# FFN-in of a hybrid backbone layer: sums of products accumulated in PSUM, weight sums and low parts on VectorE, the gate's g·sigmoid(g) as one ScalarE function

## The chip, the cores and the metric

The kernel runs on one core of one Trainium2 chip. The metric is device microseconds of one execution. Three runs of the kernel before took 1524.94, 1530.69 and 1537.96 us; their median, 1530.69 us, is the time before. All profile rows come from one profiled execution with a span of 1529.1 us.

## The reference, cut to what matters

One layer of a trunk over 512 latent tokens (and 256 context tokens) of width 1024, in float32. Three token mixers come first and end in an output projection. Then comes the sub-layer that the change touches, and a last RMSNorm:

```
def _swiglu(h, w_in, w_out):
    g, u = jnp.split(h @ w_in, 2, axis=-1)
    return (jax.nn.silu(g) * u) @ w_out

h_lat = _rmsnorm(x_lat, norm_ffn_w[l]) * (1.0 + sc2) + sh2
x_lat = x_lat + g2 * _swiglu(h_lat, w_ffn_in[l], w_ffn_out[l])
```

The hidden width is 2816, so w_in is 1024 x 5632 and gives 22 blocks of 128 columns of g and 128 of u.

## The kernel before, in words

Every float32 product is made of three TensorE products in the faster float32r type: a value is split into a high part (a cast, by ScalarE) and a low part (value minus high part, a subtraction), and high·high, high·low and low·high are summed in PSUM.

FFN-in (in `run`, from L1735 on) treats the 22 blocks of columns in two ways. The first two (FC = 2) are plain products (`halves`). The other 20 use a scheme of Strassen's kind with seven products instead of eight. A block's weights are four quadrants A11, A12, A21, A22 of 128 x 512 (the columns of g or of u by half of the channels); the tokens come in quadrants too, and sums of token quadrants are made once (`token_sums`). For each block the four weight quadrants are loaded by DMAs (L1628, issued on SP's queue), `weight_sums` makes S1 to S4 from them (L1635), and `part` splits each of the seven left operands with a cast (L1806, ScalarE) and a low part (L1807). Which engine makes the sums is given by `FE1`, which makes the low parts by `FE2`, in the order of the products; before, all four sums and two low parts of seven are on GpSimd (G), five low parts on VectorE (V).

`prepare` is a generator that is advanced once after each product. It makes the sums about a block ahead and the split of the product that stands FD = 4 places further on. The split parts and weights live in 23 slots (`wslot`, `wput`), taken in the order in which they were freed; a DMA into a slot waits for the slot's last reader.

`product` (L1842) runs 12 matmuls of 256 columns on TensorE, four channel blocks by three parts, into a PSUM bank. In the kernel before each of the seven products starts a bank of its own, and the sums that the scheme needs afterwards are VectorE's: ScalarE copies the first product to SBUF (L1858), VectorE adds the others in seven additions of 128 x 256 (L1859 to L1866), six of which read PSUM. Then `gate` (L1766) computes silu(g)·u: ScalarE's Tanh of g/2 (L1769), and two VectorE operations with a scalar and two tensors each (L1770, L1772). Blocks from FE0 = 4 on are split into high and low parts only after the loop (L362, L363), in tiles that held the tokens and the activations before; earlier ones at once. Then FFN-out starts (L1884).

TensorE runs its instructions in the order in which the code is written. For the other engines the tile framework plans the order, by the order of the code and by what its plan believes to be ready; each engine then runs that order strictly, and an instruction that waits holds all behind it on its engine. The framework places all waits, those for a buffer's last reader too.

Of the kernel before, what the change touches and what calls it, by code (L numbers as in the profile page):

```python
# [9 lines left out]
F32 = mybir.dt.float32  # L10
# [4 lines left out]
OP = mybir.AluOpType  # L15
# [25 lines left out]
KV = 6  # L41
# [15 lines left out]
FE1 = "GGGG"  # L57
FE2 = "VVGVVGV"
# [34 lines left out]
class Slots:  # L93
    """A unit's share of the working tiles of phase one; what it puts back it can take again."""
# [18 lines left out]
    def pieces(self, c):  # L113
        """A tile of class c, cut into tiles of 512 columns."""
        t = self.get(c)
        return [t[:, j:j + 512] for j in range(0, SIZE[c] - 511, 512)]
# [11 lines left out]
    def close(self, *keep):  # L128
        """Everything is given back but for the tiles kept."""
        names = {t.tensor.name for t in keep}  # L130
        for n in [n for n in self.out if n not in names]:
            c, i = self.out.pop(n)
            self.net.free[c].append(i)
        for c, z in self.own.items():
            self.net.free[c].extend(z)
            z.clear()


class Net:
# [18 lines left out]
    def crow(self, name, n):  # L158
        """A row of constants on every partition."""
        t = self.cp.tile([128, n], F32, name="c_" + name)  # L160
        self.dma(t, self.a[name].unsqueeze(0).to_broadcast([128, n]))
        return t
# [36 lines left out]
    def block(self, key):  # L199
        """The weight block of a key, split; fetched before if it was announced."""  # L200
        if key not in self.wcache:
            self.fetch(key)
        for f in self.wcache[key][3]:
            f()
        self.wcache[key][3].clear()
        return self.wcache[key][:2]

    def fetch(self, key, now=True, pieces=None):
        """Starts to load a weight block, or some pieces of it; gives the functions that split them."""
# [35 lines left out]
    def jobs(self, queue, gens=None, then=()):  # L245
        """Runs jobs (weight block, function, ...) in order, the next block on its way, and
        carries the scans on between them."""
# [36 lines left out]
    def ready(self):  # L284
        """The next job: of those that can run, the first whose weights are here."""
        z = self.upcoming()
        if not z:
            return None
        if z[0][0] is not None and z[0][0] not in self.wcache:
            z = [y for y in z if y[0] and y[0][0] in FILL and y[0] in self.wcache] + z  # L290
        return self.queue.index(z[0])

    def push(self, jobs):
        """Jobs to be run next, behind those of the block that is on its way."""
        i = max((n + 1 for n, z in enumerate(self.queue) if z[0] in self.wcache), default=0)
        self.queue[i:i] = jobs
# [15 lines left out]
    def dense(self, *parts, ks=None):  # L312
        """parts: (PSUM, weights, first column, last, tokens (high, low), first, last)."""
# [23 lines left out]
    def load_x(self):  # L337
        """The residual stream, where the context was."""
# [8 lines left out]
    def tok(self, W, i):  # L347
        """Tokens of tile i (context 0, 1, latents 2..5) on partitions, 256 columns."""
# [23 lines left out]
    def rstd_gen(self, sq, n, scale, cb, rb):  # L372
        """1 / rms of n tokens, on every partition (in rb), from tiles of squares."""
# [25 lines left out]
    def silu_c(self, c):  # L399
        """c (1 + tanh(c / 2)) of the two modulation vectors, on every partition; rows of 128, an  # L400
        identity behind them."""
# [18 lines left out]
    def modulate(self, k, s, silu):  # L420
        """Shift and scale of channels 128 k .. of one vector, by VectorE."""
# [14 lines left out]
    def modulate_pe(self, sc, ws):  # L436
        """Shift and scale of the channels from 128 KV of both vectors, by TensorE."""
# [20 lines left out]
    def scale_in(self, x, n, s, k, H, L, rb, eng):  # L458
        """The modulated norm of channels 128 k .., split."""
# [13 lines left out]
    def conv(self, acc, p, n, w, cc):  # L473
        """SAME convolution of 5 taps over the free axis, scaled by 1/2."""
# [16 lines left out]
    def gates(self):  # L491
        """Columns: decays of the SSD heads, forward and backward (32), of the mLSTM heads (8); the
        latter's input gates behind them. Tokens on partitions, tiles 0, 1 context, 2..5 latents."""
# [154 lines left out]
    def turn_rows(self, own, R, E, n, name):  # L648
        """Two sets of columns as rows over the latents, in DRAM."""
# [379 lines left out]
    def head_turn(self, own, ht, w, columns):  # L1029
        """Channels of a head on partitions, times the norm's gain; from column to row order."""  # L1030
# [257 lines left out]
    def prepare(self, b, Y, H, L, own):  # L1288
        """Splits the output of branch b, channels as they come."""
# [100 lines left out]
    def rstd2(self, c):  # L1390
        """1 / rms of 256 tokens from c on, from the sums of squares."""
# [4 lines left out]
    def late(self):  # L1396
        """The rest of the modulation of the latents."""
# [18 lines left out]
    def startup(self):  # L1416
        """The modulated inputs, and block after block of their channels the first products."""
# [144 lines left out]
    def add_square(self, m, x, c0, c1):  # L1562
        """Adds block m of the channels to the sum of squares, the last one kept apart."""
# [8 lines left out]
    def scale2(self, c, sv, h):  # L1572
        """The modulated norm before the FFN of 256 tokens from c on, in h and split."""
# [15 lines left out]
    def token_sums(self, h):  # L1589
        """With B11, B12 / B21, B22 the quadrants (channels, tokens) of h: T1 = B12 - B11,  # L1590
        T2 = B22 - T1, T3 = B22 - B12 and T4 = B21 - T2, split; per pair of channel blocks
        the tiles (T1, T3) and (T4, T2)."""
# [17 lines left out]
    def weight_sums(self, f, out):  # L1610
        """The quadrants (columns, channels) A11, A12 / A21, A22 of an FFN block and
        S1 = A21 + A22, S2 = S1 - A11, S3 = A11 - A21, S4 = A12 - S2, in steps."""
# [27 lines left out]
    def aup(self, up):  # L1640
        """The decays' weights of a head, three times: their low parts once and the high ones twice."""
# [5 lines left out]
    def small(self, p, c0, c1):  # L1647
        """The rows of the decays, three times: their high parts twice and the low ones."""
# [5 lines left out]
    def first(self, Y):  # L1654
        """Ends the products of the startup: the rows of the gates, the first GLA head's q and k."""
# [20 lines left out]
    def run(self):  # L1676
# [19 lines left out]
        with pool("hx") as self.hp:  # L1696
# [45 lines left out]
            with pool("sp3") as sp, pool("fp") as fp:  # L1742
# [12 lines left out]
                def split(f):  # L1755
                    """An early block in tiles of its own, a late one where h and the block before were."""
# [9 lines left out]
                def gate(f, g, u):  # L1766
                    """silu(g) u"""
                    t = sp.tile([128, 512], F32, name="ft", bufs=2)
                    S.activation(t, g, AF.Tanh, scale=0.5)  # L1769
                    V.scalar_tensor_tensor(t, t, 1.0, g, op0=OP.add, op1=OP.mult)  # L1770
                    act[f] = t if f < FE0 else fp.tile([128, 512], F32, name=f"a{f}")
                    V.scalar_tensor_tensor(act[f], t, 0.5, u, op0=OP.mult, op1=OP.mult)  # L1772
# [4 lines left out]
                order = ("A11", "S2", "S1", "A12", "S3", "A22", "S4")  # L1777
# [4 lines left out]
                def prepare():  # L1782
                    """Sums and splits of the weights, one step ahead of each product."""
# [29 lines left out]
                def halves():  # L1813
                    """The first FFN blocks, half of the tokens after the other."""
# [27 lines left out]
                def product(f, n, dst):  # L1842
                    dst = dst[:, :256]
                    H, L, slots = parts.pop(7 * (f - FC) + order.index(n))
                    for k in range(4):
                        h, l = B[n][k]
                        w, v = H[:, 128 * k:128 * k + 128], L[:, 128 * k:128 * k + 128]
                        for j, (x, y) in enumerate(((w, h), (w, l), (v, h))):
                            T.matmul(dst, x, y, start=(k == 0 and j == 0), stop=(k == 3 and j == 2))  # L1849
                    self.wput(*slots)  # L1850
                    next(prep, None)
                    return dst

                for f in range(FC, KF):
                    lo, hi = slice(0, 256), slice(256, 512)
                    g, u = (sp.tile([128, 512], F32, name=n, bufs=2) for n in ("fg", "fu"))
                    m, r, v = (sp.tile([128, 256], F32, name=n, bufs=2) for n in ("fm", "fr", "fv"))
                    S.copy(m, product(f, "A11", self.acc_bank()))  # L1858
                    V.tensor_add(r, m, product(f, "S2", self.bank()))  # L1859
                    p5 = product(f, "S1", self.bank())  # L1860
                    V.tensor_add(g[:, lo], m, product(f, "A12", self.acc_bank()))
                    V.tensor_add(g[:, hi], r, p5)
                    V.tensor_add(v, r, product(f, "S3", self.bank()))
                    V.tensor_add(u[:, hi], v, p5)
                    V.tensor_add(u[:, lo], v, product(f, "A22", self.acc_bank()))
                    V.tensor_add(g[:, hi], g[:, hi], product(f, "S4", self.bank()))  # L1866
                    gate(f, g, u)
# [46 lines left out]
    def final(self, c):  # L1914
        """The last norm of 256 tokens from c on; the gain is in but for the last block of channels."""
# [4 lines left out]
        for h in range(4):  # L1920
            o = self.sp.tile([128, 2, 256], F32, name=("ft", "fu")[h % 2], bufs=2)
# [34 lines left out]
def lay_out(i):  # L1956
# [43 lines left out]
    # constants of the shapes alone  # L2000
# [29 lines left out]
```

## Time and profile before

| | |
|---|---|
| median of three runs | 1530.69 us (1524.94 to 1537.96) |
| span of the profiled execution | 1529.1 us |
| TensorE (PE) busy | 1406.8 us, 92% |
| VectorE (DVE) busy | 1033.0 us, 68% |
| ScalarE (ACT) busy | 644.0 us, 42% |
| GpSimd (POOL) busy | 587.2 us, 38% |
| mean granted TensorE clock | 0.973 of full speed |

The shares are means over stages. A matmul counts as busy from its start to a modelled end, and matmuls overlap: one of 256 columns is listed with some 0.28 us, while the next starts 0.118 us later. So TensorE's speed is read from the count of matmuls in a stretch, not from the busy time. In the same way a VectorE or ScalarE instruction's listed time overlaps the next one's; the spacing of starts is what an instruction costs in a full queue.

### The profile page before, as it was taken

How to read it: one execution, taken by the hardware profiler on the slowest of the kernel's cores; microseconds unless marked ns; L12 is line 12 of the kernel's file. 1: busy time of each engine (PE TensorE's matmuls, PEld its weight loads, DVE VectorE, ACT ScalarE, POOL GpSimd, SP SyncE). 2: the span in 40 equal slices, each digit the busy share in tenths (PEclk: the TensorE clock that was granted, in tenths of full speed). 3: DMA queues.
4: the chain of work that ended last, by engine and by line, in shares of the span. 5: the costliest groups of instructions: out<-in, count | busy, mean ns of one | idle time of the engine just before them, and what ended most of it. 6: DMA issues, size and time to landing. Idle time of an engine off the chain costs nothing.

```text
span 1529.1 us, 22249 instructions
## 1 busy us (share of the span) xinstructions
PE 1406.8 (92%) x8044; PEld 1204.6 (79%) x8044; DVE 1033.0 (68%) x1783; ACT 644.0 (42%) x1191; POOL 587.2 (38%) x465
## 2 busy tenths in 40 slices
PE   5898999999999999998997789899998888888997
PEld 3687889887788886887796767677798888887887
DVE  7958463869684658786666765435369999999332
ACT  4464464553244443334454443333355343436231
POOL 4423432324222123221226353134457888881011
PEclk9998999999999999999999999999989999999999
DMA  6532323233443234354455566666322233223331
GB/s 258 189 105 84 106 69 97 72 97 97 137 126 103 78 96 129 88 129 127 159 173 171 175 210 211 197 201 215 117 77 83 83 94 100 84 84 113 90 90 66
DMA packets 99022, 190.39 MB, mean 125 GB/s; under 512 B 10752, under 2 KB 19472, under 8 KB 97760
## 3 DMA queue, kind: packets, MB, share of 16 engines
q1 hardware_dynamic: 98912, 188.97, 39.8%
q8 instruction: 63, 1.03, 0.3%
q14 instruction: 47, 0.39, 0.1%
HBM read 167.27 MB, written 21.14 MB: 123 GB/s over the span
## 4 chain that ended last, share of the span: by engine, by line
PE 53%; DVE 19%; DMA 8%; issue 6%; ACT 5%; POOL 4%; SPq 0%; DVEq 0%; ACTq 0%; POOLq 0%
PE acc L318 28%; PE acc L1884 7%; PE acc L357 7%; DVE w L1807 6%; DMA w<-in_w_main_dram 4%; PE bank L318 2%; DVE ft L1770 2%; DMA w<-in_w_b_dram 1%; ACT w L1806 1%; ACT w L215 1%; DVE w L217 1%; DMA t<-in_wmodT_dram 1%; PE bank L974 1%; POOL row L1160 1%; DMA gd<-xk 1%
## 5 line engine op out<-in xcount | busy, mean ns | idle before, releaser
L217 POOL TENSOR_TENSOR w<-w,w 128x512 fp32r<-128x512 f32 x125 | 176.2, 1409 | 572.8 <-ACT w L215 499.4
L318 PE MATMUL acc<-hlh,w 128*128 128x512 f32 (+1 forms) x1160 | 390.7, 406 | 5.5 <-ACT hlh L465 1.9
L215 ACT CAST w<-w 128x512 fp32r<-128x512 f32 (+1 forms) x302 | 183.2, 613 | 382.9 <-DMA w<-in_w_main_dram 182.6
L217 DVE TENSOR_TENSOR w<-w,w 128x512 fp32r<-128x512 f32 x177 | 138.6, 785 | 202.7 <-ACT w L215 168.6
L318 PEld LDWEIGHTS acc<-hlh,w 128*128 128x128 f32 x1160 | 225.3, 194 | 59.9 <-ACT hlh L465 2.2
L318 PE MATMUL acc<-hll,w 128*128 128x512 f32 (+1 forms) x576 | 230.7, 400 | 3.7 <-DVE hll L471 1.5
L1635 POOL TENSOR_TENSOR w<-w,w 128x512 f32<-128x512 f32 x80 | 135.7, 1717 | 2.7 <-DMA w<-in_w_ffs_dram 1.9
L318 PEld LDWEIGHTS acc<-hll,w 128*128 128x128 f32 x576 | 111.8, 194 | 28.7 <-DVE hll L471 1.9
L1807 DVE TENSOR_TENSOR w<-w,w 128x512 fp32r<-128x512 f32 x100 | 124.0, 1241 | 0.0
L318 PE MATMUL acc<-t,w 128*128 128x512 f32 x440 | 111.2, 401 | 7.4 <-DVE t L363 2.7
L318 PEld LDWEIGHTS acc<-t,w 128*128 128x128 f32 x440 | 83.2, 190 | 28.9 <-DVE t L363 4.3
L1806 ACT CAST w<-w 128x512 fp32r<-128x512 f32 x140 | 79.1, 618 | 60.9 <-DVE w L1807 50.2
L357 PE MATMUL acc<-w,hlh 128*128 128x256 f32 x512 | 96.6, 289 | 0.0
L1849 PE MATMUL bank<-th,w 128*128 128x256 f32 x480 | 93.4, 283 | 0.1
L1849 PE MATMUL acc<-hlh,w 128*128 128x256 f32 x280 | 59.6, 290 | 29.9 <-DVE w L1807 29.9
L357 PEld LDWEIGHTS acc<-w,hlh 128*128 128x128 f32 x512 | 81.6, 194 | 3.0 <-ACT t L920 1.6
L480 DVE SCALAR_TENSOR_TENSOR cacc<-acc,c_scanc,cacc 128x510 f32<-128x510 f32 (+3 forms) x124 | 77.7, 631 | 6.7 <-ACT cacc L476 5.8
L1849 PEld LDWEIGHTS bank<-th,w 128*128 128x128 f32 x480 | 77.3, 190 | 0.5 <-DVE w L1807 0.3
L1807 POOL TENSOR_TENSOR w<-w,w 128x512 fp32r<-128x512 f32 x40 | 61.5, 1538 | 38.1 <-ACT w L1806 36.2
L357 PE MATMUL acc<-w,hll 128*128 128x256 f32 x256 | 73.4, 287 | 0.0
L1849 PEld LDWEIGHTS acc<-hlh,w 128*128 128x128 f32 x280 | 46.0, 190 | 33.7 <-DVE w L1807 33.7
L1849 PE MATMUL bank<-tl,w 128*128 128x256 f32 x240 | 67.8, 282 | 0.0
(453 smaller groups left out, 3089.5 us busy)
## 6 DMA issues: line engine op xcount, KB each, us to landing
w<-in_w_main_dram SPq DMA_DIRECT2D x180, 256.0 KB, 3.4
w<-in_w_ffs_dram SPq DMA_DIRECT2D x80, 256.0 KB, 3.1
t<-in_wmodT_dram SPq DMA_DIRECT2D x32, 512.0 KB, 4.0
w<-in_w_b_dram SPq DMA_DIRECT2D x48, 256.0 KB, 3.5
xk<-gd SPq DMA_DIRECT2D x40, 256.0 KB, 3.5
w<-in_w_ffo_dram SPq DMA_DIRECT2D x40, 256.0 KB, 2.6
row<-rows SPq DMA_DIRECT2D x16, 512.0 KB, 5.5
wmod<-in_wmod_dram SPq DMA_DIRECT2D x6, 1024.0 KB, 8.3
```

The lines of the kernel that those rows point to most:

```text
L215: self.S.copy(h, w)
L217: self.LE[self.wcount % len(self.LE)].tensor_sub(l, w, h.bitcast(F32))
L318: self.T.matmul(dst, w[:, m0:m1], x[:, c0:c1], start=(k == 0 and j == 0), stop=(k == nk - 1 and j == 2))
L357: self.T.matmul(p, x[:, t0:t0 + 128], w, start=(k == 0 and j == 0), stop=(k == KT - 1 and j == 2))
L480: V.scalar_tensor_tensor(acc[:, o0:o1], p[:, o0 + d:o1 + d], w[:, cc, j:j + 1], acc[:, o0:o1], op0=OP.mult, op1=OP.add)
L974: T.matmul(bs[:, :257], kw[d], v[:, 2 + i], start=True, stop=True)
L1635: getattr(next(eng), op)(new(z), x, y)
L1770: V.scalar_tensor_tensor(t, t, 1.0, g, op0=OP.add, op1=OP.mult)
L1806: S.copy(H, x)
L1807: le[p % 7].tensor_sub(L, x, H.bitcast(F32))
L1849: T.matmul(dst, x, y, start=(k == 0 and j == 0), stop=(k == 3 and j == 2))
L1884: T.matmul(po, w, x[:, c0:c1], start=(f == 0 and j == 0), stop=(f == KF - 1 and j == 2))
```

## The change

Three things change, all in FFN-in. (1) `FE1` and `FE2` name VectorE throughout: no weight sum and no low part of the 20 blocks is on GpSimd any more. (2) The products are put in another order and share PSUM banks: A11, S2, S3 and A22 accumulate in one bank X, S1 and S4 in a second, Y; A12 has a third, Z. ScalarE copies X out after A11, S2 and S3 and Y after S1. VectorE's additions shrink to three (two read PSUM), and u's first half is read by the gate from X directly. (3) `gate` uses ScalarE's Silu of g and a plain VectorE product with each half of u. The tile `fu` goes, `fp` comes. All other lines of the diff are comments and docstrings.

```
-FE1 = "GGGG"
-FE2 = "VVGVVGV"
+FE1 = "VVVV"
+FE2 = "VVVVVVV"
...
-                def gate(f, g, u):
+                def gate(f, g, *u):
...
                     t = sp.tile([128, 512], F32, name="ft", bufs=2)
-                    S.activation(t, g, AF.Tanh, scale=0.5)
-                    V.scalar_tensor_tensor(t, t, 1.0, g, op0=OP.add, op1=OP.mult)
+                    S.activation(t, g, AF.Silu)
                     act[f] = t if f < FE0 else fp.tile([128, 512], F32, name=f"a{f}")
-                    V.scalar_tensor_tensor(act[f], t, 0.5, u, op0=OP.mult, op1=OP.mult)
+                    c = 0
+                    for z in u:
+                        cs = slice(c, c + z.shape[-1])
+                        V.tensor_mul(act[f][:, cs], t[:, cs], z)
+                        c = cs.stop
...
-                order = ("A11", "S2", "S1", "A12", "S3", "A22", "S4")
+                order = ("A11", "S1", "S2", "A12", "S3", "S4", "A22")
...
-                def product(f, n, dst):
-                    dst = dst[:, :256]
+                def product(f, n, dst, first=True):
...
-                            T.matmul(dst, x, y, start=(k == 0 and j == 0), stop=(k == 3 and j == 2))
+                            T.matmul(dst, x, y, start=(first and k == 0 and j == 0), stop=(k == 3 and j == 2),
+                                     skip_group_check=True)
...
-                    g, u = (sp.tile([128, 512], F32, name=n, bufs=2) for n in ("fg", "fu"))
-                    m, r, v = (sp.tile([128, 256], F32, name=n, bufs=2) for n in ("fm", "fr", "fv"))
-                    S.copy(m, product(f, "A11", self.acc_bank()))
-                    V.tensor_add(r, m, product(f, "S2", self.bank()))
-                    p5 = product(f, "S1", self.bank())
-                    V.tensor_add(g[:, lo], m, product(f, "A12", self.acc_bank()))
-                    V.tensor_add(g[:, hi], r, p5)
-                    V.tensor_add(v, r, product(f, "S3", self.bank()))
-                    V.tensor_add(u[:, hi], v, p5)
-                    V.tensor_add(u[:, lo], v, product(f, "A22", self.acc_bank()))
-                    V.tensor_add(g[:, hi], g[:, hi], product(f, "S4", self.bank()))
-                    gate(f, g, u)
+                    g = sp.tile([128, 512], F32, name="fg", bufs=2)
+                    m, r, v, p5 = (sp.tile([128, 256], F32, name=n, bufs=2) for n in ("fm", "fr", "fv", "fp"))
+                    X, Y, Z = (z[:, :256] for z in (self.acc_bank(), self.bank(), self.bank()))
+                    product(f, "A11", X)
+                    S.copy(m, X)
+                    product(f, "S1", Y)
+                    S.copy(p5, Y)
+                    product(f, "S2", X, False)
+                    S.copy(r, X)
+                    product(f, "A12", Z)
+                    V.tensor_add(g[:, lo], m, Z)
+                    product(f, "S3", X, False)
+                    S.copy(v, X)
+                    product(f, "S4", Y, False)
+                    V.tensor_add(g[:, hi], r, Y)
+                    V.tensor_add(v, v, p5)
+                    product(f, "A22", X, False)
+                    gate(f, g, X, v)
```

## Rows read from the trace of the kernel before

**Rows 1.** Busy time of each engine in stretches of the span: the stretch in us, its length, busy us (and count) of PE, PEld, DVE, ACT and POOL, granted TensorE clock, DMA share, GB/s. The first stretch is the FFN-in loop's beginning, the others lie in its middle; the second runs from one stall of TensorE to the next.

```profile
1154.60:1165.00 10.40, 6.24 (x38) 6.15 (x39) 0.84 0.31 102
...
1194.00:1204.00 10.00, 10.00 (x84) 9.86 (x84) 9.97 (x15) 4.58 (x9) 8.87 (x6) 1.00 0.25 77
1200.00:1250.00 50.00, 44.10 (x366) 43.28 (x366) 49.83 (x59) 20.72 (x40) 42.35 (x26) 1.00 0.31 95
```

(The first row is of the loop's matmuls alone: PE, PEld, clock, DMA share, GB/s.)

**Rows 2.** Who waited for whom in the loop (1160 to 1391 us): the waiting engine, tile and line, the releaser; us in total, times, longest. The last row is of the DMA queue's own waits.

```profile
ACT ft L1769 <- DVE fg L1866: 62.1, 19, 5.2
PE acc L1849 <- DVE w L1807: 25.8, 18, 1.7
...
SPq L1628 <- DVE w L1807: 169.8, 20, 9.9
```

**Rows 3.** TensorE's instructions in order of time: the loop's start and first stall, the first matmul of a product S2 and that of the product A12 two products (24 matmuls) later, two of the stalls that come back once in a block (twelve blocks apart), and the loop's last matmuls. Start, us, engine, line, operation, count; in brackets the idle time before and its releaser.

```profile
1154.72 0.28 PE L1849 MATMUL acc<-hlh,w 128*128 128x256 f32 x1
...
1159.15 0.51 PE L1849 MATMUL acc<-hlh,w 128*128 128x256 f32 x2 [4.04 <-DVE w L1807]
...
1230.22 0.28 PE L1849 MATMUL bank<-th,w 128*128 128x256 f32 x1
...
1233.05 0.28 PE L1849 MATMUL acc<-hlh,w 128*128 128x256 f32 x1
...
1240.64 0.50 PE L1849 MATMUL acc<-hlh,w 128*128 128x256 f32 x2 [1.52 <-DVE w L1807]
...
1380.98 0.51 PE L1849 MATMUL acc<-hlh,w 128*128 128x256 f32 x2 [1.52 <-DVE w L1807]
...
1390.61 0.52 PE L1849 MATMUL bank<-sq,w 128*128 128x256 f32 x3
```

**Rows 4.** VectorE and GpSimd in the loop, groups by line and form (VectorE from 1177 to 1369 us, GpSimd's sums from 1050 to 1430 us): busy us, mean ns of one, idle before.

```profile
L1807 DVE TENSOR_TENSOR w<-w,w 128x512 fp32r<-128x512 f32 x82 | 102.4, 1249 | 0.0
L1770 DVE SCALAR_TENSOR_TENSOR ft<-ft,fg 128x512 f32<-128x512 f32 x17 | 29.2, 1716 | 0.0
...
L1635 POOL TENSOR_TENSOR w<-w,w 128x512 f32<-128x512 f32 x80 | 135.7, 1717 | 2.7 <-DMA w<-in_w_ffs_dram 1.9 <-DVE w L217 0.6
```

**Rows 5.** VectorE and GpSimd in order of time in one block of the loop.

```profile
1234.91 5.13 POOL L1635 TENSOR_TENSOR w<-w,w 128x512 f32<-128x512 f32 x3
1241.95 1.30 POOL L1807 TENSOR_TENSOR w<-w,w 128x512 fp32r<-128x512 f32 x1 [1.91 <-ACT w L1806]
...
1238.84 1.75 DVE L1807 TENSOR_TENSOR w<-w,w 128x512 fp32r<-128x512 f32 x1
1240.85 0.68 DVE L1807 TENSOR_TENSOR w<-w,w 128x512 fp32r<-128x512 f32 x1
1241.45 0.41 DVE L1862 TENSOR_TENSOR fg<-fr,bank 128x256 f32<-128x256 f32 x1
1241.78 0.41 DVE L1861 TENSOR_TENSOR fg<-fm,acc 128x256 f32<-128x256 f32 x1
```

**Rows 6.** VectorE in order of time behind the loop, where GpSimd does nothing.

```profile
1398.52 0.68 DVE L363 TENSOR_TENSOR a<-a,hlh 128x512 fp32r<-128x512 f32 x1
1399.12 0.68 DVE L1772 SCALAR_TENSOR_TENSOR a<-ft,fu 128x512 f32<-128x512 f32 x1
...
1402.73 0.41 DVE L217 TENSOR_TENSOR w<-w,w 128x256 fp32r<-128x256 f32 x1
1403.07 0.68 DVE L363 TENSOR_TENSOR a<-a,hlh 128x512 fp32r<-128x512 f32 x1
```

**Rows 7.** ScalarE in order of time: the table load before the first gate, and one block of the loop.

```profile
1158.07 1.28 ACT L1769 ACT_TABLE_LOAD   x1
...
1229.49 2.18 ACT L1806 CAST w<-w 128x512 fp32r<-128x512 f32 x4
1234.82 0.63 ACT L1769 ACTIVATE ft<-fg 128x512 f32<-128x512 f32 x1 [3.15 <-DVE fg L1866]
1235.36 0.36 ACT L1858 COPY fm<-acc 128x256 f32<-128x256 f32 x1
1235.61 0.62 ACT L1806 CAST w<-w 128x512 fp32r<-128x512 f32 x1
```

**Rows 8.** Two handovers in order of time, from TensorE to a waiting ScalarE and from ScalarE to a waiting TensorE.

```profile
1119.28 0.95 PE L377 MATMUL bank<-ones,hll 128*128 128x1 f32 x8
1120.27 0.26 ACT L380 ACTIVATE rcol<-bank,eps 128x2 f32<-128x2 f32 x1 [2.68 <-PE bank L377]
...
1124.23 0.59 ACT L1585 ACTIVATE hlh<-a,mod,sv 128x256 fp32r<-128x256 f32 x1
1124.88 0.38 PE L318 MATMUL acc<-hlh,w 128*128 128x256 f32 x1 [1.48 <-ACT hlh L1585]
```

**Rows 9.** Ahead of the loop, in order of time: VectorE's low parts of the first weights and its first one of the loop, GpSimd's first three sums.

```profile
1130.12 4.10 DVE L217 TENSOR_TENSOR w<-w,w 128x512 fp32r<-128x512 f32 x4
1157.35 1.75 DVE L1807 TENSOR_TENSOR w<-w,w 128x512 fp32r<-128x512 f32 x1
...
1132.02 4.60 POOL L1635 TENSOR_TENSOR w<-w,w 128x512 f32<-128x512 f32 x3 [0.63 <-DVE w L217]
```

**Rows 10.** TensorE's first stalls in FFN-out, in order of time.

```profile
1392.01 0.50 PE L1884 MATMUL acc<-ah,w 128*128 128x512 f32 x1 [0.88 <-ACT w L215]
...
1393.71 0.73 PE L1884 MATMUL acc<-ah,w 128*128 128x512 f32 x2 [0.97 <-DVE w L217]
```

More of the change, by code (lines that the diff above doesn't have):

```diff
@@ L1848, in product @@
                         for j, (x, y) in enumerate(((w, h), (w, l), (v, h))):
-                            T.matmul(dst, x, y, start=(k == 0 and j == 0), stop=(k == 3 and j == 2))
+                            T.matmul(dst, x, y, start=(first and k == 0 and j == 0), stop=(k == 3 and j == 2),
+                                     skip_group_check=True)
                     self.wput(*slots)
                     next(prep, None)
-                    return dst
                 for f in range(FC, KF):
                     lo, hi = slice(0, 256), slice(256, 512)
-                    g, u = (sp.tile([128, 512], F32, name=n, bufs=2) for n in ("fg", "fu"))
-                    m, r, v = (sp.tile([128, 256], F32, name=n, bufs=2) for n in ("fm", "fr", "fv"))
-                    S.copy(m, product(f, "A11", self.acc_bank()))
-                    V.tensor_add(r, m, product(f, "S2", self.bank()))
-                    p5 = product(f, "S1", self.bank())
-                    V.tensor_add(g[:, lo], m, product(f, "A12", self.acc_bank()))
-                    V.tensor_add(g[:, hi], r, p5)
-                    V.tensor_add(v, r, product(f, "S3", self.bank()))
-                    V.tensor_add(u[:, hi], v, p5)
-                    V.tensor_add(u[:, lo], v, product(f, "A22", self.acc_bank()))
-                    V.tensor_add(g[:, hi], g[:, hi], product(f, "S4", self.bank()))
-                    gate(f, g, u)
+                    g = sp.tile([128, 512], F32, name="fg", bufs=2)
[16 more added lines that the diff above has]
+                    gate(f, g, X, v)
                 for f in range(FE0, KF):
@@ L1920, in final @@
         for h in range(4):
-            o = self.sp.tile([128, 2, 256], F32, name=("ft", "fu")[h % 2], bufs=2)
+            o = self.sp.tile([128, 2, 256], F32, name=("ft", "fg")[h % 2], bufs=2)
             for j in range(2):
```

## Prediction

> **What bounds the kernel now.** I read the stage table first, then the waits, then the order of time. The change lives in the FFN-in loop, which runs from 1154.72 to about 1391.0 us, 236.3 us for 20 blocks [rows 3]. In its middle VectorE is busy 49.83 of 50 us and GpSimd 42.35, while ScalarE is busy 20.72 and TensorE issues 366 matmuls [rows 1]. A fed TensorE would issue 420: 84 of them (one block's seven products of 12) take 10.00 us between two stalls [rows 1], and inside a product the pitch is 2.83/24 = 0.118 us [rows 3]. What TensorE waits for is always a low part of VectorE's [rows 2], once in a block, behind the second matmul of A11. The block period is (1380.98 - 1240.64)/12 = 11.70 us [rows 3]. So VectorE's queue sets the period, and TensorE loses 1.70 us of each 11.70.
>
> Why is VectorE full? Its low parts take 1249 ns on average and its two gate operations some 1.7 us each [rows 4], yet the same low part takes 1.75 us when it lies beside a GpSimd sum and 0.68 us in the 1.9 us in which GpSimd was idle [rows 5]. Behind the loop, with GpSimd idle throughout, all of them, the gate's form with two tensors too, take 0.68 us, at a pitch of 0.60 [rows 6]. GpSimd's work thus makes VectorE's more than twice as long. Additions that read PSUM keep their 0.41 us, pitch 0.33, while GpSimd works [rows 5].
>
> **The change, part by part, per block.**
>
> VectorE. Eleven operations on two SBUF tensors of 128x512 (four sums, seven low parts) at the undisturbed pitch of 0.60 us [rows 6]: 6.60 us. Three additions and two gate products of 128x256 at 0.33 [rows 5] (0.34 where both inputs are in SBUF [rows 6]): 1.66 us. Sum 8.3 us, against 11.7 before. What leaves is the two gate operations of 1.7 us, four of seven additions and all of the stretching.
>
> ScalarE. Seven casts at (2.18 - 0.62)/3 = 0.52 us, the function at 0.54 and four copies at 0.25 instead of one [rows 7]: 5.2 us of 10. No row shows Silu. The lower bound is the Tanh's 0.54 pitch in its place, the upper one a table load of 1.28 us for each Silu and each following cast; I take the Tanh's, because casts ran behind the loop's single load without another [rows 7]. The upper bound makes 5.2 + 2 x 1.28 = 7.8 us, still under 10.
>
> TensorE. The 1680 matmuls stay. New are waits: S2, S3 and A22 start accumulating in X only when ScalarE has copied X out, after A11, S2 and S3. Between the end of the one and the start of the next lies one product in another bank, 12 x 0.118 = 1.41 us, of which the last matmul's tail (0.28 - 0.12) must be taken off: 1.25 us. A copy needs 0.04 us to start, 0.36 to run [rows 7], and TensorE 0.06 to follow [rows 8]: 0.46, or 0.98 if it meets a cast that has just begun. So the wait costs nothing while ScalarE is not itself held; behind a held S2 all of TensorE would stand. S4's wait for Y has two more products between. VectorE's additions wait for Z, Y and X; queued behind them are the next sums and low parts, which are four products (5.6 us) ahead of their use, so I cost that wait at nothing too; below nothing it can't go.
>
> SP's queue. The same 80 DMAs in the same order, each waiting for a slot's last reader, most of all a low part [rows 2]. Slots come free in the same pattern; at 10 us a block the DMA share goes from 0.30 to 0.30 x 11.7/10 = 0.35 [rows 1]. Cost nothing.
>
> With VectorE at 8.3, ScalarE at 5.2 and TensorE at 10.0, TensorE becomes the bound. What is late next is nothing in steady state.
>
> **The first products.** TensorE stands 4.04 us before the loop's third matmul [rows 3], because VectorE is still busy with the token sums; then its granted clock is low for a while (0.84 in the stretch) and 38 matmuls take 10.40 us [rows 1] instead of 38 x 0.118 = 4.5: 5.9 us lost. VectorE takes over four sums and one low part here, 5 x 0.60 = 3.0 us, and is rid of stretching: the four low parts of 4.10 us beside GpSimd's first sums [rows 9] become 4 x 0.60, and the first one of the loop goes from 1.75 [rows 9] to 0.68: 2.8 us. I take zero, with -5.9 and +3 as the ends.
>
> So the loop should take 20 x 10.0 + 5.9 = 205.9 us instead of 236.3: 30.4 us less.
>
> **Behind the loop** TensorE stands 0.88 + 0.97 us for weights that VectorE and ScalarE still owe [rows 10]. VectorE's backlog shrinks, but the splits of the late activations still wait for the loop's last products. I take 1 us of gain, with 0 and 1.9 as ends.
>
> Sum: 1529.1 - 30.4 - 1.0 = 1497.7 for an execution like the profiled one, whose span is 1.6 us under the median; for the median I predict **1499 us**.
>
> **A rule against the change.** Starts of undisturbed VectorE operations of 0.68 us lie 0.60 apart [rows 6]. The Trainium skill, "VectorE: DVE Perf Modes", section "The DRAIN you can't avoid", says that each operation is followed by a drain of about its duration less 266 ns before the next one starts. By that rule a low part would cost 0.68 + 0.41 us, eleven of them 12 us with the additions on top, VectorE would be the bound at some 14.8 us a block, and the kernel would be slower by about 60 us. The rows contradict it, so it gets a chance of 0.01, inside "slower".
>
> **Rivals.**
>
> *ScalarE's copies hold TensorE in part.* ScalarE runs a fixed order. If copies of X come behind two casts, or behind a cast whose sum VectorE has not yet made, each is late by some 0.3 us: 3 x 0.3 x 20 = 18 us given back, 1517; with half of it 1508. For: before, ScalarE spent 62.1 us waiting for VectorE with its gate function at the head of the queue [rows 2], and the copy of A11 ran right behind it [rows 7]. Against: that wait came from VectorE's backlog, which goes. Chance 0.14 (1507 to 1517).
>
> *They hold it fully: slower.* Should Silu, at the head of ScalarE's queue, still wait 3.15 us for g [rows 7] with the copy of the next A11 behind it, then S2 starts 3.15 + 0.54 + 0.46 - 1.25 = 2.9 us late in every block, 58 us in all: 1499 + 58 = 1557. The mechanism decides from 30.4/20 = 1.5 us per block on. Against: g's last addition now follows S4, one product before the block ends, so Silu runs during A22. With the drain rule, chance 0.06.
>
> *VectorE remains the bound.* If operations on SBUF tensors keep part of their length with GpSimd idle, say 0.80 us, VectorE needs 11 x 0.80 + 1.66 = 10.5 us a block, 1509; at 0.90 us 11.6, no gain, 1531. Against: every row with GpSimd idle shows 0.68 [rows 5, 6]. Chance 0.09 for 1517 to 1545, together with whatever else leaves the period where it was (the change not doing what it says).
>
> *The start's loss goes as well*: 1499 - 5.9 = 1493, down to 1490 at a pitch of 0.118 instead of 10.0/84. Chance 0.08.
>
> **How the numbers follow.** The forecast (1493 to 1507) gets 0.63. The range 1489 to 1517 holds the forecast, the partial rival and the better start, 0.85, less a little for the spread of runs (1525 to 1538 before). Within 1%, about 15 us, is what a measurement of this kernel can tell from no change; faster than that means under 1515: 0.63 + 0.08 + most of 0.14 = 0.85; same 0.09; slower 0.06.
>
> **What would show it.** Right: in the loop's middle 84 matmuls in each 10 us with the granted clock at 1.00, GpSimd without work, VectorE's low parts and sums at 0.68 us with about 17% of idle time, released by TensorE's products; ScalarE's copies starting within 0.6 us of their product's end; no waits of TensorE for them. Wrong: TensorE waiting for a copy of X in each block (the ScalarE rivals), low parts over 0.75 us or VectorE without idle time (the bound stays), a first stall much over 4 us or a longer way into FFN-out (the ends mis-sized).

## The result, and the profile after

The changed kernel takes 1492.6 us (median of four runs, 1490.09 to 1499.72) against 1529.2 us before: ratio 0.9763, interval 0.974 to 0.9786, so 36.6 us faster. The forecast was 1499, the range 1489 to 1517. A second measurement of the same kernel gave 0.9774 (0.9741 to 0.9806).

First the stage table of the changed kernel. Columns: stretch, length, busy us (count) of PE, PEld, DVE, ACT and POOL, granted clock, DMA share, GB/s. The stretches are the loop's beginning, two of its middle, and the step into FFN-out.

```profile
1147.00:1160.00 13.00, 8.80 (x60) 8.46 (x60) 12.11 (x20) 9.53 (x18) 1.21 (x2) 0.87 0.35 98
1200.00:1250.00 50.00, 50.00 (x425) 50.00 (x424) 42.93 (x80) 30.07 (x60) 0.00 (x0) 1.00 0.36 107
1250.00:1300.00 50.00, 50.00 (x425) 50.00 (x424) 43.01 (x80) 30.08 (x60) 0.00 (x0) 1.00 0.36 107
1350.00:1365.00 15.00, 15.00 (x83) 12.88 (x83) 14.30 (x27) 11.03 (x23) 0.00 (x0) 1.00 0.45 136
```

Where TensorE had 366 matmuls in 50 us [rows 1], it now has 425; both counts take in the two or three that were running when the stretch began, so the period is read from the order of time below. VectorE was busy 99.7% and is busy 86%; GpSimd has nothing to do. VectorE's groups from 1170 to 1340 us (line, form, count; busy us, mean ns; idle before and its releaser) show why:

```profile
L1810 DVE TENSOR_TENSOR w<-w,w 128x512 fp32r<-128x512 f32 x122 | 82.8, 686 | 5.0 <-ACT w L1809 4.6
L1635 DVE TENSOR_TENSOR w<-w,w 128x512 f32<-128x512 f32 x69 | 47.0, 682 | 0.0
L1869 DVE TENSOR_TENSOR fg<-fm,bank 128x256 f32<-128x256 f32 x17 | 7.2, 421 | 16.7 <-PE bank L1852 16.7
```

A low part takes 686 ns where it took 1249 [rows 4], a weight sum 682 ns where GpSimd took 1717. And VectorE's idle time is now released by TensorE (16.7 us before the addition that reads Z): the direction of the wait in [rows 2] has turned round.

In order of time (start, us, engine, line), TensorE at the loop's two ends and at the last matmul of two products A11, eleven blocks apart, and ScalarE around one boundary between blocks:

```profile
1147.76 0.28 PE L1852 MATMUL acc<-hlh,w 128*128 128x256 f32 x1
...
1152.36 0.50 PE L1852 MATMUL acc<-hlh,w 128*128 128x256 f32 x2 [4.20 <-DVE w L1810]
...
1235.73 0.29 PE L1852 MATMUL acc<-hlh,w 128*128 128x256 f32 x1
...
1345.31 0.28 PE L1852 MATMUL acc<-hlh,w 128*128 128x256 f32 x1
...
1353.80 0.28 PE L1852 MATMUL acc<-th,w 128*128 128x256 f32 x1
1353.92 0.39 PE L1893 MATMUL acc<-ah,w 128*128 128x512 f32 x1
...
1233.76 0.63 ACT L1769 ACTIVATE ft<-fg 128x512 f32<-128x512 f32 x1
...
1236.06 0.38 ACT L1863 COPY fm<-acc 128x256 f32<-128x256 f32 x1 [0.81 <-PE acc L1852]
```

The loop runs from 1147.76 to 1353.9 us: 206.1 us instead of 236.3 [rows 3]. A block takes (1345.31 - 1235.73)/11 = 9.96 us instead of 11.70. The product that ends at 1235.73 + 0.29 = 1236.02 us is copied out from 1236.06 on; behind the first block no product waits for a copy by more than 0.18 us. FFN-out follows without a gap and takes 1488.3 - 1353.9 = 134.4 us instead of 138.1. That is 33.9 us. The other 6.9 of the 40.8 us between the two profiled spans lie before the loop, where nothing that TensorE executes has changed.

### The profile page after: what moved, and what is told of

Read it like the earlier page. It is cut to its first block, busy times and chain, and to the rows that moved or that the text cites. A ratio compares the mean times of both kernels' runs of the same rounds, so it can differ in the third digit from the quotient of the medians.

```text
span 1488.3 us, 22056 instructions
## 1 busy us (share of the span) xinstructions
PE 1395.2 (94%) x8044; PEld 1198.5 (81%) x8044; DVE 975.6 (66%) x1821; ACT 668.0 (45%) x1251; POOL 394.1 (26%) x345
## 5 line engine op out<-in xcount | busy, mean ns | idle before, releaser
L217 POOL TENSOR_TENSOR w<-w,w 128x512 fp32r<-128x512 f32 x125 | 176.8, 1415 | 567.0 <-ACT w L215 473.1
L318 PEld LDWEIGHTS acc<-hlh,w 128*128 128x128 f32 x1160 | 222.1, 192 | 58.8 <-ACT hlh L465 2.2
L217 DVE TENSOR_TENSOR w<-w,w 128x512 fp32r<-128x512 f32 x177 | 137.1, 778 | 198.8 <-ACT w L215 163.0
L1810 DVE TENSOR_TENSOR w<-w,w 128x512 fp32r<-128x512 f32 x140 | 94.5, 685 | 5.0 <-ACT w L1809 4.6
L1852 PE MATMUL acc<-th,w 128*128 128x256 f32 x480 | 95.6, 282 | 0.2 <-ACT fm L1863 0.2
L1568 POOL TENSOR_TENSOR sq<-sq,sq 128x512 f32<-128x512 f32 x6 | 7.8, 1297 | 308.1 <-ACT sq L1566 308.1
L1852 PEld LDWEIGHTS acc<-th,w 128*128 128x128 f32 x480 | 77.8, 188 | 0.7 <-ACT fm L1863 0.4
L1852 PE MATMUL acc<-tl,w 128*128 128x256 f32 x240 | 67.3, 280 | 0.0
L1411 DVE SCALAR_TENSOR_TENSOR xk<-t 128x1024 bf16<-128x1024 f32 x32 | 44.3, 1385 | 29.4 <-DMA t<-in_wmodT_dram 29.4
L318 PE MATMUL acc<-row,w 128*128 128x512 f32 (+1 forms) x312 | 63.3, 360 | 0.0
L318 PEld LDWEIGHTS acc<-row,w 128*128 128x128 f32 x312 | 52.1, 188 | 9.7
```

The lines of the kernel that those rows point to most:

```text
L217: self.LE[self.wcount % len(self.LE)].tensor_sub(l, w, h.bitcast(F32))
L318: self.T.matmul(dst, w[:, m0:m1], x[:, c0:c1], start=(k == 0 and j == 0), stop=(k == nk - 1 and j == 2))
L1411: V.scalar_tensor_tensor(junk, w, 0.5, sc, op0=OP.mult, op1=OP.mult, accum_out=self.mod[:, 0, j:j + 1])
L1568: self.G.tensor_add(a, a, t)
L1810: le[p % 7].tensor_sub(L, x, H.bitcast(F32))
L1852: T.matmul(dst, x, y, start=(first and k == 0 and j == 0), stop=(k == 3 and j == 2), skip_group_check=True)
```

## The experiments

Loop and FFN-out are read from the traces (first to last matmul of `product`, and from there to the end); before they are 236 and 138 us.

| kernel | ratio to before (interval) | loop us | FFN-out us |
|---|---|---|---|
| changed kernel, twice | 0.9763 (0.974 to 0.9786), 0.9774 (0.9741 to 0.9806) | 206, 206 | 134, 135 |
| e1 engines only | 0.9816 (0.9775 to 0.9857) | 209 | 140 |
| e2 banks only | 0.9962 (0.9934 to 0.999) | 235 | 134 |
| e3 Silu only | 0.9823 (0.9776 to 0.987) | 210 | 141 |
| e4 engines undone | 0.9881 (0.9838 to 0.9923) | 223 | 134 |
| e5 Tanh in the changed kernel | 0.9782 (0.9766 to 0.9799) | 205 | 134 |
| e6 sums on GpSimd | 0.9934 (0.9916 to 0.9952) | 228 | 134 |
| e7 low parts on GpSimd | 0.9853 (0.9831 to 0.9874) | 211 | 134 |
| e8 copies exposed | 0.9981 (0.996 to 1.0002) | 237 | 134 |
| e9 early splits | 0.9783 (0.9752 to 0.9813) | 206 | 135 |
| e10 early splits, token sums on VectorE | 0.9738 (0.9709 to 0.9767) | 202 | 134 |

**e1, the engines alone** (on the kernel before):

```
-FE1 = "GGGG"
-FE2 = "VVGVVGV"
+FE1 = "VVVV"
+FE2 = "VVVVVVV"
```

> Only the weight sums and low parts go to VectorE; the additions, the order of products and the Tanh gate stay as before. Lock theory (a GpSimd operation and a VectorE operation with two SBUF tensors exclude each other; before, the period is 6 x 1.25 us of GpSimd + 7 x 0.60 us of VectorE = 11.7 us): with GpSimd idle VectorE needs 11 x 0.60 + 7 x 0.33 + 2 x 0.60 = 10.1 us a block, TensorE 10.0, so the period is 10.1 to 10.3 us and nearly the whole gain of the change is there: 1495 to 1502 us, ratio to before 0.978 to 0.983. Rival (the banks and copies or the gate carry the gain): ratio 0.995 to 1.00.

Measured 0.9816. The stage table's row of 100 us of the loop:

```profile
1210.00:1310.00 100.00, 100.00 (x830) 98.58 (x829) 100.00 (x197) 49.22 (x89) 0.00 (x0) 1.00 0.36 106
```

From the first matmul of one block to that of the next TensorE takes 10.15 us: VectorE is full (100.00), but no fuller than TensorE. VectorE's low parts in the loop (1170 to 1345 us), with nothing else changed than that GpSimd is idle, take 694 ns where they took 1249 [rows 4], and the gate operations 693 and 695:

```profile
L1807 DVE TENSOR_TENSOR w<-w,w 128x512 fp32r<-128x512 f32 x120 | 83.3, 694 | 0.0
```

Taking GpSimd away gives 27.5 of the loop's 30 us by itself.

**e2, the banks alone** (on the changed kernel):

```
-FE1 = "VVVV"
-FE2 = "VVVVVVV"
+FE1 = "GGGG"
+FE2 = "VGVVVVG"
...
-                    S.activation(t, g, AF.Silu)
+                    S.activation(t, g, AF.Tanh, scale=0.5)
+                    V.scalar_tensor_tensor(t, t, 1.0, g, op0=OP.add, op1=OP.mult)
...
-                        V.tensor_mul(act[f][:, cs], t[:, cs], z)
+                        V.scalar_tensor_tensor(act[f][:, cs], t[:, cs], 0.5, z, op0=OP.mult, op1=OP.mult)
```

> Only the accumulation in shared banks, the four copies and the new order; sums and two low parts of seven on GpSimd as before, Tanh gate. Lock theory: 6 x 1.25 of GpSimd + VectorE's two-SBUF work of 5 x 0.60 + 0.34 (v + p5) + 0.60 (t, g) + 0.34 (second half of the gate's product) = 11.8 us a block: no gain, ratio 0.998 to 1.005. Mean-duration theory (each VectorE operation has a fixed longer time beside GpSimd, as the prediction's rows list them): 5 x 1.25 + 3 x 0.33 + 0.9 + 1.7 + 0.33 + 0.9 = 11.1 us, ratio about 0.992.

Measured 0.9962, between the two. The period in the middle is 11.0 us (two stalls of TensorE, at 1235.45 and 1246.48 us), the number that mean durations gave, but not for their reason: VectorE is busy 87.7 of 100 us and so does not set it. Some 10 us of the gain are lost again in the first blocks. The limit is a new one, seen in order of time:

```profile
1234.51 0.62 ACT L1810 CAST w<-w 128x512 fp32r<-128x512 f32 x1 [1.75 <-POOL w L1635]
1235.03 0.36 ACT L1868 COPY fr<-acc 128x256 f32<-128x256 f32 x1
...
1235.45 0.39 PE L1853 MATMUL acc<-th,w 128*128 128x256 f32 x1 [0.80 <-ACT fr L1868]
```

ScalarE stands at a cast whose sum GpSimd has not finished; the copy of X is behind it; TensorE waits for the copy. This is the prediction's ScalarE rival, in a kernel that keeps GpSimd.

**e3, Silu alone** (on the kernel before):

```
-                    S.activation(t, g, AF.Tanh, scale=0.5)
-                    V.scalar_tensor_tensor(t, t, 1.0, g, op0=OP.add, op1=OP.mult)
+                    S.activation(t, g, AF.Silu)
...
-                    V.scalar_tensor_tensor(act[f], t, 0.5, u, op0=OP.mult, op1=OP.mult)
+                    V.tensor_mul(act[f], t, u)
```

> Only the gate: Silu on ScalarE and one product of 128x512 on VectorE; all else as before. Lock theory: one two-SBUF operation of 0.60 us less, 6 x 1.25 + 6 x 0.60 = 11.1 us a block, 20 x 0.6 = 12 us less, ratio 0.992. Mean-duration theory: one operation of 1.7 us less, 10.0 us a block, ratio 0.978 to 0.982. If Silu reloaded tables or ran longer than Tanh: Silu rows over 0.65 us or a table load in each block, ratio over 1.

Measured 0.9823. The row of 100 us, and one group:

```profile
1215.00:1315.00 100.00, 99.95 (x826) 98.15 (x824) 100.00 (x126) 46.19 (x88) 97.95 (x60) 1.00 0.32 106
```

```profile
L1771 DVE TENSOR_TENSOR a<-ft,fu 128x512 f32<-128x512 f32 x10 | 17.1, 1715 | 0.0
```

The period, from first matmul to first matmul, is 10.2 us. Taking one VectorE operation away saved 1.5 us a block, not 0.60: beside GpSimd such an operation costs nearly what it is listed with, 1.7 us. My lock theory, with turns of 1.25 and 0.60 us, falls here and in e2; that its sum fitted the 11.7 us before is no support for it. VectorE (100.00) and GpSimd (97.95) are both full here; which of them sets the 10.2 us, no run shows.

**e4, the engines undone** (on the changed kernel; FE1 and FE2 as in e2):

> The changed kernel with the four sums and two low parts of seven (S1's and A22's) back on GpSimd. Lock theory: 6 x 1.25 + 5 x 0.60 + 0.34 + 0.34 = 11.2 us a block, 10 us less than before, ratio about 0.993; VectorE again without idle time beside GpSimd or in turns with it. Mean-duration theory: VectorE 5 x 1.25 + 3 x 0.33 + 2 x 0.9 = 9.0 us, GpSimd 10 us, TensorE 10 us: period 10.0 to 10.3, ratio 0.976 to 0.982.

Measured 0.9881, a miss for both: 10.6 us a block. Banks and Silu together are worth 13 us of loop. VectorE has idle time (it is busy 79 of 100 us), and TensorE again waits for copies of X behind a cast that waits for GpSimd:

```profile
1232.84 0.62 ACT L1809 CAST w<-w 128x512 fp32r<-128x512 f32 x1 [1.33 <-POOL w L1635]
1233.37 0.37 ACT L1867 COPY fr<-acc 128x256 f32<-128x256 f32 x1
...
1233.79 0.39 PE L1852 MATMUL acc<-th,w 128*128 128x256 f32 x1 [0.37 <-ACT fr L1867]
```

VectorE's gate in one block, with GpSimd at work throughout:

```profile
1239.03 1.51 DVE L1774 TENSOR_TENSOR a<-ft,fv 128x256 f32<-128x256 f32 x1
1240.46 0.41 DVE L1774 TENSOR_TENSOR a<-ft,acc 128x256 f32<-128x256 f32 x1
```

The same product of 128x256, once with both inputs in SBUF (1.51 us) and once with one in PSUM (0.41). With GpSimd idle, in the changed kernel, the one with both inputs in SBUF takes 0.42 us too. The Trainium skill, "SBUF — State Buffer", section "Who interferes with whom", says that a VectorE instruction with two SBUF inputs contends with a GpSimd one that reads SBUF, and that one with at most one SBUF input does not, outside its two-port modes; the two rows agree.

**e5, Tanh in the changed kernel** (the gate's lines as in e2, engines as changed):

> The changed kernel with the gate before (Tanh, and two-tensor operations with a scalar on VectorE). Slack theory (TensorE is the bound, VectorE has some 1.6 us a block to spare): VectorE's block grows by one operation of 0.60 us to about 8.9 us, under TensorE's 10.0, so the loop stays at 206 us and the ratio to before at 0.976. Rival (Silu carries a part of its own): ratio 0.98 or more.

Measured 0.9782, loop 205 us: Silu adds nothing once the engines and banks are changed. VectorE's busy share rises from 86% to 93%, which is slack used and no time.

**e6 and e7, one half of the engine move each** (on the changed kernel):

```
-FE1 = "VVVV"
+FE1 = "GGGG"
```

> The changed kernel with the four weight sums on GpSimd, all low parts on VectorE. Theory H (what GpSimd does to the changed kernel is that ScalarE stands at a cast whose sum GpSimd has not made, with a copy of X behind it): TensorE waits for copies of X in each block, period 10.3 to 10.9 us, ratio 0.982 to 0.99. Theory S (only VectorE's stretching counts: 7 x 0.60 + 1.66 + at most 4 x 1.05 = 10.1 us): period 10.0 to 10.1, no waits for copies, ratio 0.976 to 0.979.

```
-FE2 = "VVVVVVV"
+FE2 = "VGVVVVG"
```

> The changed kernel with the low parts of S1 and A22 on GpSimd, all sums on VectorE. Theory H: no cast waits for GpSimd, so no copy of X is late; VectorE has 9 x 0.60 + 1.66 + at most 2 x 1.05 = 9.2 us: the period stays at 10.0, loop 206 us, ratio 0.976. Rival (any two-SBUF work of GpSimd beside VectorE costs TensorE time): ratio 0.98 or more.

e6 measured 0.9934, 10.9 us a block, on theory H's side and beyond its range. Its rows in order of time:

```profile
1230.77 0.62 ACT L1809 CAST w<-w 128x512 fp32r<-128x512 f32 x1 [1.65 <-POOL w L1635]
1231.30 0.37 ACT L1867 COPY fr<-acc 128x256 f32<-128x256 f32 x1
...
1231.71 0.38 PE L1852 MATMUL acc<-th,w 128*128 128x256 f32 x1 [0.68 <-ACT fr L1867]
...
1234.79 6.26 POOL L1635 TENSOR_TENSOR w<-w,w 128x512 f32<-128x512 f32 x4 [4.65 <-PE bank L1852]
```

GpSimd waits 4.65 us for a slot that a product frees, then makes all four sums in a row; they are late, the cast waits, the copy behind it waits, TensorE waits. GpSimd is idle nearly half the time, and more of its work makes the kernel faster (e4): what matters is which queue its results stand ahead of. e7 measured 0.9853; its middle goes at TensorE's pace,

```profile
1153.00:1166.00 13.00, 7.86 (x44) 7.84 (x44) 12.78 (x19) 9.39 (x17) 4.74 (x4) 0.74 0.33 103
1213.00:1313.00 100.00, 100.00 (x847) 100.00 (x847) 95.47 (x142) 61.28 (x121) 28.25 (x20) 1.00 0.34 106
```

847 matmuls in 100 us, but the loop as a whole takes 5.1 us more than the changed kernel's: 4.0 in its first three blocks (a first stall of 5.14 us, 44 matmuls in 13 us) and 1.1 in its last two. Theory H holds for the steady state, with no wait there for a copy; the ratio lies where the rival had it, by these 5.1 us and some 5 more that lie before the loop, already at the norm before FFN, which the edit doesn't reach.

**e8, copies exposed** (on the changed kernel; the calls of `product` follow the order, with each copy right behind its product):

```
-                order = ("A11", "S1", "S2", "A12", "S3", "S4", "A22")
+                order = ("A11", "S2", "S1", "A12", "S3", "A22", "S4")
```

> The changed kernel with the products in the order before (A11, S2, S1, A12, S3, A22, S4) and the same shared banks: S2 follows A11 in X at once, and A22 follows S3, so two copies of four stand bare. Prediction's price of a bare copy: tail 0.16 + start 0.04 + copy 0.37 + 0.06 = 0.63 us, up to 1.15 where it meets a cast: 1.3 to 2.3 us a block, loop 232 to 252 us, ratio 0.993 to 1.007. If the wait is hidden by other means (TensorE's queue running ahead): loop 206 us, ratio 0.976.

Measured 0.9981, loop 237 us, 11.4 us a block. Two of TensorE's waits in order of time:

```profile
1229.90 0.39 PE L1852 MATMUL acc<-th,w 128*128 128x256 f32 x1 [0.46 <-ACT fv L1871]
1230.12 0.28 PE L1852 MATMUL acc<-tl,w 128*128 128x256 f32 x1
...
1234.91 0.39 PE L1852 MATMUL acc<-th,w 128*128 128x256 f32 x1 [0.51 <-ACT fm L1863]
```

With the tail of 0.16 that the listed idle time leaves out these are 0.62 and 0.67 us, near the 0.63 worked out. The price leaves one thing out: the next matmul starts 0.22 us later instead of 0.118, some 0.11 us more. So a wait costs 0.27 us beyond its listed idle time, and the two make up the 1.5 us by which a block is longer than the changed kernel's 9.96. (Silu now stands right ahead of the copy of A11; it makes that copy 0.06 us later.) With the banks shared, the order of the products alone decides over 31 us, the loop's whole gain.

**e9 and e10, the loop's beginning.** e9 (on the changed kernel) writes the splits of A11 and A12 of the first block ahead of the token sums, and puts A12 second (its calls follow the order); e10 also moves GpSimd's token sums to VectorE:

```
-                order = ("A11", "S1", "S2", "A12", "S3", "S4", "A22")
+                order = ("A11", "A12", "S2", "S1", "S3", "S4", "A22")
...
-                    for _ in self.weight_sums(FC, sums[FC]):
-                        pass
-                    for p in range(FD):
-                        part(p)
-                    yield
+                    gen = self.weight_sums(FC, sums[FC])
+                    next(gen)
+                    part(0)
+                    part(1)
+                    yield
+                    for _ in gen:
+                        pass
+                    part(2)
+                    part(3)
+                    yield
...
+                            next(prep)
                             self.ts = self.token_sums(hk)
                             next(prep)
```

```
-            G.tensor_sub(b12, b22, b12)
+            V.tensor_sub(b12, b22, b12)
...
-            G.tensor_sub(b21, b21, b22)
+            V.tensor_sub(b21, b21, b22)
```

> The changed kernel with the products in the order A11, A12, S2, S1, S3, S4, A22 (no copy of X bare) and the first block's splits of A11 and A12 written ahead of the token sums, which they don't need. TensorE then has two products, 2.8 us, before it needs the token sums. If the first stall is VectorE's order of work: the 4.2 us shrink to about 2.9 us, at another place, the loop takes 203 to 205 us. If it is VectorE's amount of work that counts, and the token sums end later by the 1.2 us moved ahead: 4 us of stall stay, loop 206 us. Ratio within 0.002 of the changed kernel either way.

> As the run before, with the eight token sums that GpSimd makes on VectorE too: 8 x 0.33 = 2.7 us more work there, some 4.8 us less of stretching (the VectorE rows of 0.85 to 1.81 us in that stretch against 0.41 and 0.68 alone). The first stall should fall by 2 us more, to about 1 us; loop 200 to 203 us, ratio 0.001 to 0.003 under the changed kernel's. If VectorE is already full there and only gains work: the stall grows, loop 207 us or more.

e9 measured 0.9783, loop 206 us: no gain, but not for the reason written. The 4.2 us went and another stall came, for the copy of A11; e9's rows in order of time, and then e10's:

```profile
1147.34 0.62 ACT L1604 CAST th<-a 128x512 fp32r<-128x512 f32 x1 [2.40 <-POOL a L1598]
...
1157.33 0.36 ACT L1869 COPY fm<-acc 128x256 f32<-128x256 f32 x1
...
1157.74 0.58 PE L1858 MATMUL acc<-th,w 128*128 128x256 f32 x1 [5.21 <-ACT fm L1869]
```

```profile
1151.08 0.37 ACT L1869 COPY fm<-acc 128x256 f32<-128x256 f32 x1
...
1151.50 0.39 PE L1858 MATMUL acc<-th,w 128*128 128x256 f32 x1 [1.68 <-ACT fm L1869]
```

The copy's place in ScalarE's queue is behind casts of token sums that wait for GpSimd (2.40 us), the table load, the first gates, and a weight cast that waits 0.80 us for VectorE. With the token sums on VectorE the stall falls to 1.68 us (about 1 was expected), a second of 0.67 comes, and the loop takes 202 us, 4 less. e10 has the lowest ratio of all, 0.9738, but its interval overlaps that of the changed kernel beside it (0.9774): the loop's gain is in the trace, the total is not settled.

**The changed kernel again**, beside e9 and e10:

> The changed kernel again, unaltered. If the 6.9 us by which the loop began earlier in the first profiled execution is spread of the executions and not the change's, the loop begins somewhere between 1147 and 1155 us here too; the loop itself takes 205 to 206 us and FFN-out 134 to 135 us again. If it is the change's, the loop begins at 1147 to 1149 us. Ratio to before 0.974 to 0.980.

Measured 0.9774, loop 206.0 us from 1149.5 us on, FFN-out 134.6 us: what loop and FFN-out gain repeats. Where the loop begins lies hardly outside the 1147 to 1149 us of the second reading, so this alone does not tell the two apart; the stretch ahead of the loop does for a part of it, as shown below.

## Why the prediction was right, point by point

**The bound.** Right: VectorE's queue set 11.70 us, and with 8.3 us of work in it (8.6 measured, 86% of a block) TensorE's 10.0 became the period (9.96 measured; the 84 matmuls in 10.00 us [rows 1] were counted to the last one's listed end). The loop was forecast at 205.9 us and took 206.1, twice. That it came so close is partly luck: the period made 0.8 us less of the 20 blocks, and the loop's beginning lost 206.1 - 20 x 9.96 = 6.9 us instead of 5.9.

**Handovers and ScalarE.** The copy's 0.04 us start was met, and its price, bare, in e8 but for 0.11 us. Silu takes 0.63 us as Tanh did, with one table load before the first gate and none behind it in the loop, so the lower bound was the right one; ScalarE's 5.2 us a block became 6.0 (30.07 of 50 us busy), still far from 10. Both ScalarE rivals stayed away in the changed kernel, but their mechanism is real: e2, e4 and e6 show it in each block, e9 in the first, where ScalarE's queue holds a cast that waits for GpSimd ahead of a copy. In e2, e4 and e6 TensorE's listed waits for the copy of X behind S2 come to 0.78, 0.37 and 0.69 us a block; with the 0.27 us of e8 on top of each, and the 9.96 us, they make 11.0, 10.6 and 10.9 us, the measured periods. So in these three kernels that wait is the whole loss of the loop's middle. I had feared a late sum of VectorE's, or a late g, instead.

**The first products.** 4.04 us of stall became 4.20, and the first block takes 16.3 us instead of 15.8: half a microsecond where zero was taken.

**Behind the loop.** This term was mis-sized: 1 us was taken, 1.9 as the end, 3.7 measured. I counted the first two stalls by their listed 0.88 and 0.97 us [rows 10]; from start to start they cost 2.4. And I left out the later ones, which wait for splits of late activations and cost 1.3. All of them went. It is the banks' part: FFN-out takes 134 us in every kernel that has them, with GpSimd at work or not, and 138 to 141 in those without (before, e1, e3). Why the banks do it is argued, not tested alone: VectorE leaves the loop with less of its gate and additions still to do.

**The rest.** Loop and FFN-out explain 33.9 of the 36.6 us; by the second ratio, 0.9774, there are 34.4 us to explain. The profiled executions differ by 6.9 us more before the loop. Of these, 4.3 are there already at the first instruction of the norm before FFN (1123.69 us before, 1119.35 after). No change reaches it, and among all kernels it lies anywhere from 1117.7 to 1126.5 us. The other 2.6 us lie between the norm and the loop: this stretch (columns as in the stage table) in the kernel before, in the changed kernel and in its second profile.

```profile
1124.14:1154.70 30.56, 28.58 (x202) 28.17 (x203) 26.66 (x44) 17.85 (x38) 23.18 (x24) 0.83 0.20 62
1119.79:1147.76 27.97, 25.98 (x202) 25.57 (x203) 25.42 (x47) 18.54 (x39) 18.02 (x21) 0.94 0.21 68
1118.86:1149.46 30.60, 28.68 (x202) 28.27 (x203) 25.44 (x47) 18.55 (x39) 17.90 (x21) 0.83 0.20 63
```

At the same granted clock of 0.83 the changed kernel takes as long there as the kernel before, so the 2.6 us are spread of the executions. I put the 4.3 down to it too; that some part of them belongs to the change is not excluded.

**What the sum hid.** I costed the change as a whole and it holds as a whole, but its parts don't add. In the loop the engines alone are worth 27.5 us, Silu alone 26.6, the banks alone about 1, all three 30. Either of the first two takes VectorE from 11.7 to nearly TensorE's 10; the second of them to come finds next to nothing left. The banks depend on the engines: on top of Silu, with sums on GpSimd, they cost 14 us of loop (e3 to e4, 210 to 223); on top of the engines they give 3.6 us of loop and 5 of FFN-out (e1 to e5).

One sum in the prediction is wrong: at a pitch of 0.118 us the better start ends at 1491 us, not at 1490; nothing hangs on it.

**The drain rule** would have made the block 14.8 us; it did not come. VectorE in order of time in the changed kernel, a sum, a low part and a sum:

```profile
1235.52 0.68 DVE L1635 TENSOR_TENSOR w<-w,w 128x512 f32<-128x512 f32 x1
1236.12 0.68 DVE L1810 TENSOR_TENSOR w<-w,w 128x512 fp32r<-128x512 f32 x1
1236.72 0.68 DVE L1635 TENSOR_TENSOR w<-w,w 128x512 f32<-128x512 f32 x1
```

The starts lie 0.60 us apart, less than the listed duration of one.

## What to carry to other kernels

Before giving work to a second engine, price what its presence does to the first: here GpSimd's 197 us of sums and low parts stretched VectorE's low parts from 0.68 to 1.25 us on average, and removing either the sharer or one stretched operation came close to the next bound (10.15 and 10.2 us a block against 9.96). When PSUM banks are reused across products, put a product in another bank between a copy and its successor, and see that nothing in the copying engine's queue ahead of the copy waits for a slow engine. Parts of a change that relieve the same queue don't add up: the next bound, here TensorE's 10 us a block, caps them all.

## What the runs showed of the hardware that I had not expected

An operation of 0.60 us on VectorE was worth 1.5 us of period beside GpSimd (e3: 11.70 to 10.2 us), and a product of 128x256 took 1.51 us with both inputs in SBUF against 0.41 with one in PSUM (e4). Over the 13 us that hold the stall of 4.2 us at the loop's start TensorE's granted clock was 0.87; over the 13 us of e7 that hold its stall of 5.14 us it was 0.74, against 1.00 in the middle of both loops.
